# Sparse attention maps in a written-out order, gate weights loaded a chunk ahead, no GpSimd work among the mixers' weights

## The chip, the cores and the metric

The kernel runs on one core of a Trainium2 chip. A core has five engines with instruction queues of their own: PE (TensorE, matrix products), DVE (VectorE), ACT (ScalarE), POOL (GpSimd) and SP (SyncE, which here issues the DMAs). Each takes its instructions in order; an instruction that waits holds up all that stand behind it on its engine. The metric is device time in microseconds (us) of one execution; the kernel before takes 1821.24 us (median of 3 runs).

## The reference, cut to what matters

One decoder layer on 512 tokens of width 1024, in float32. The change is in its first part, two token mixers and their merge:

```python
u = rms_norm(h, norm_mix)
qa, ka, va, qb, kvb, gb, gate_a, gate_b = split(u @ w_in)
o_a = diff_attention(qa, ka, va, ...)      # 4 heads, two causal maps each: a = softmax(s0) - lam * softmax(s1)
o_b = nsa_attention(qb, kvb, sigmoid(gb))  # 8 heads in 2 groups: compressed, selected and window branch
#   o_b = g0 * o_cmp + g1 * o_slc + g2 * o_win      (with 8 blocks and top-16, all blocks are selected:
#   selected and window branch are plain causal attention with keys and values of their own)
merged = sigmoid(gate_a) * (o_a @ w_branch_a) + sigmoid(gate_b) * (o_b @ w_branch_b)
h = h + merged @ w_out
h = h + cross_attention(...); h = h + peer_ffn(...); out = rms_norm(h)
```

## The kernel before, in words

Every projection is done with operands split in two: `h` is the value rounded to TensorE's float32r, `l` the rest, and a product is three matmuls (`mm3`, lines 89 to 91: h·h, l·h, h·l). `split` (line 80) makes the pair: a cast on ACT and a subtraction on DVE, or on POOL for the weights whose running number stands in `WPOOL` and for the masks where a call says so. `wload` brings a weight chunk of 2048 columns in two halves: DMA to `wr`, cast to `wh`, subtraction to `wl`.

The mixers run in stages, the times being those of the profile. Norm and transposes of the input (to about 25 us); first projections and the hidden layer of the compressed keys (25 to 80); four differential heads (65 to 220, `diff_head`: two causal maps, the scaling P1 = P1·f (line 292) and P0 = P0·f − P1 (line 293), transposes (237), values (300), a head norm, transposes (309)), with the projections of the next head and of the sparse attention between them; the compressed map `nsa_cmp_map` (198 to 240); the sparse maps (`nsa_pair`, 201 to 372); the gates (`gate_half`, until 385); the merge with `w_br` (385 to 430). Behind that follow `w_out`, cross-attention and the expert layer, whose code is not touched.

A sparse map, for one head `r + 4g` and one branch `j`, is: four score rows of 128, 256, 384 and 512 columns (PE, line 216), each read out of PSUM by DVE with bias and row minimum (219), then exponential with row sum on ACT (220); the row factors on DVE (480, 481); the four rows scaled (487 on DVE, 485 on POOL for the rows named in `POOLM`: the third row, 384 columns); ten 128×128 transposes into three PSUM banks (PE, 237), each bank split by ACT (`PTh`) and DVE (`PTl`) (80); eight matmuls with the values (493) that add into the head's bank. After branch `j = 1` the two halves of the bank are added (`osum` on ACT, 496; add on DVE, 497). `nsa_pair` builds two heads at a time, with `GATE` halves of the gate projection (24 matmuls of 512 columns each) called between maps. Eleven of the sixteen gate halves are called there, five behind the last map; the results stay in SBUF (`gates`).

The order of instructions around here is not that of the code: outside `manual_schedule` blocks a scheduler with an estimate of durations orders the instructions of each engine, and interleaves what the dependencies allow.

Of the kernel before, what the change touches and what calls it, by code (L numbers as in the profile page):

```python
# [38 lines left out]
WPOOL = (1, 7, 9, 13, 15, 16, 17, 20, 21, 23, 38, 39, 42, 43)  # L39
DAF = ('cv', 'k', 'q', 'm')  # L40
# [3 lines left out]
POOLM = ((0, 2), (1, 2))  # L44
GATE = (3, 2, 1, 1, 1, 0, 1, 2)
# [14 lines left out]
class Kernel:  # L60
# [45 lines left out]
    def wload_parts(self, src, n=2048, eng=None):  # L106
# [9 lines left out]
        def half(c):  # L116
            r = wp.tile([P, w], F32, tag="wr", bufs=3, name=self.nm("wr"))
            nc.sync.dma_start(r, src[:, c:c + w])
            self.split(h[:, c:c + w], l[:, c:c + w], r, eng)
# [86 lines left out]
    def causal_maps(self, qk, biases):  # L206
# [4 lines left out]
        for i in range(NB):  # L211
            n, o, bl = P * (i + 1), ROW[i], slice(i * P, (i + 1) * P)
            sp = [self.bank("sc")[:, 0:n] for _ in qk]
            for s, (q, k) in zip(sp, qk):
                for y in range(2):
                    self.mark = nc.tensor.matmul(s, lhsT=q[:, bl], rhs=k[y][:, 0:n], start=y == 0, stop=y == 1)  # L216
# [6 lines left out]
    def causal_T(self, Pt, exact):  # L223
# [7 lines left out]
        for kbs, w in (((0,), 512), ((1, 3), 512), ((2,), 256)):  # L231
            pt = self.bank("pt")
# [18 lines left out]
    def diff_lambda(self, pool):  # L251
        nc = self.nc
        da = self.da
        lp = da.tile([P, 4, 64], F32, name="lamp")
        DQ(nc).dma_start(lp, self.a["lam"].unsqueeze(0).broadcast_to([P, 4, 64]))
        lt = da.tile([P, 2, 64], F32, name="lamt")
# [81 lines left out]
    def nsa_cmp_hidden(self, j, A, pool):  # L338
# [3 lines left out]
        ph = self.bank("pj")[0:32, 0:256]  # L342
# [6 lines left out]
        nc.scalar.activation(ge, ph, AF.Gelu)  # L349
        pt = self.bank("pt")  # L350
# [112 lines left out]
    def nsa_pair(self, r, fill):  # L463

        nc, dw = self.nc, self.dw
        hds, par = (r, r + 4), r % 2
        pr = slice(64 * par, 64 * par + 64)
        Bs = [self.bias(2.0 ** (-(hd + 1))) for hd in hds]
        po = [self.bank("po") for _ in hds]
        for hd, o in zip(hds, po):  # L470
            w = self.vc[:, hd].rearrange("p a b -> p (a b)")
            for y in range(2):
                nc.tensor.matmul(o, lhsT=w, rhs=self.pc[y], start=y == 0, stop=False)
        for j in range(2):
            maps = self.causal_maps([(self.qb[g][:, r, :], self.kb[j][g]) for g in range(2)], Bs)
            for _ in range(GATE[2 * r + j]):
                fill(self.mark)
            for g, (hd, o, (Pt, l)) in enumerate(zip(hds, po, maps)):
                f = dw.tile([P, NB], F32, tag="rl2", bufs=2, name=self.nm("rl"))
                nc.vector.reciprocal(f, l)  # L480
                nc.vector.tensor_tensor(f, f, self.gate[:, :, hd * 3 + 1 + j], OP.mult)
                for i in range(NB):
                    cs = slice(ROW[i], ROW[i] + P * (i + 1))
                    if (g, i) in POOLM:
                        nc.gpsimd.tensor_tensor(Pt[:, cs], Pt[:, cs], f[:, i:i + 1].broadcast_to([P, P * (i + 1)]), OP.mult)
                    else:
                        nc.vector.tensor_scalar(Pt[:, cs], Pt[:, cs], f[:, i:i + 1], None, OP.mult)
                T = self.causal_T(Pt, False)
                for kb in range(NB):
                    cs = slice(OFF[kb], OFF[kb] + S - kb * P)  # L490
                    w = self.vb[:, kb, j, g].rearrange("p z c -> p (z c)")
                    for y in range(2):
                        nc.tensor.matmul(o[:, kb * P:S], lhsT=w, rhs=T[y][:, cs], start=False, stop=(j, kb, y) == (1, NB - 1, 1))
        for hd, o in zip(hds, po):
# [14 lines left out]
    def mixers(self):  # L509
        nc, a = self.nc, self.a  # L510
        with ExitStack() as s1, ExitStack() as right:
# [30 lines left out]
            with ExitStack() as s2:  # L542
# [29 lines left out]
                for r in range(4):  # L572
                    self.nsa_pair(r, lambda m: self.gate_half(gp, m))
# [687 lines left out]
```

## Time and profile before

| | us |
|---|---|
| median of 3 runs (1819.18 to 1821.83) | 1821.24 |
| profiled execution | 1821.76 |
| its span on the core | 1820.0 |
| PE busy | 1753.3 (96%) |
| DVE busy | 1320.2 (73%) |
| ACT busy | 763.5 (42%) |
| POOL busy | 537.0 (30%) |

The ends of matmuls are modelled in this profile, so that a PE that is busy by the page need not be at its peak. The granted clock of TensorE is given as a share: 1.0 is the higher level (2.4 GHz), 0.50 the lower (1.2 GHz); its mean over the execution is 0.984. The stage in question is the first 430 us.

### The profile page before, as it was taken

The page shows a single profiled execution, that of the slowest core. Times are in us where ns is not written, and L with a number is a line of the kernel's source. Part 1 is how long each engine was busy: PE and PEld are TensorE (multiplying, and loading weights), DVE is VectorE, ACT ScalarE, POOL GpSimd, SP SyncE. Part 2 cuts the span into 40 slices and gives each one's busy share as a digit, 9 for nine tenths or more (in the row PEclk, how much of TensorE's full clock was granted, in tenths as well). Part 3 has the DMA queues.
Part 4 walks back from the last instruction along what each step waited for, and adds up shares of the span by engine and source line. Part 5 has one row for each costly group of instructions (what it writes and reads, how often), then busy time and mean ns, then how long its engine had stood idle before and what let it go on. Part 6 is the DMA issues. An engine that isn't in the chain of part 4 may idle for free.

```text
span 1820.0 us, 25916 instructions
## 1 busy us (share of the span) xinstructions
PE 1753.3 (96%) x9667; PEld 1550.2 (85%) x9667; DVE 1320.2 (73%) x2639; ACT 763.5 (42%) x1253; POOL 537.0 (30%) x386
## 2 busy tenths in 40 slices
PE   8999989999999999999999999999999999999998
PEld 7877777878987889998989888889888888888887
DVE  4465567555555899998873777778777787778777
ACT  4665446643454334454443333333233233323324
POOL 2211203100220251013210444344444444344442
PEclk8998989999999999999999999999999999999999
DMA  5521111035232224679999899999899989888994
GB/s 204 165 77 53 59 47 47 24 133 179 96 115 74 98 81 131 190 237 315 308 324 290 317 334 343 329 323 343 298 332 328 325 318 351 314 304 317 341 347 151
DMA packets 157967, 407.80 MB, mean 224 GB/s; under 512 B 13072, under 2 KB 62992, under 8 KB 157712
## 3 DMA queue, kind: packets, MB, share of 16 engines
q1 hardware_dynamic: 120976, 271.90, 42.9%
q0 software_dynamic: 36864, 134.23, 21.0%
q8 instruction: 76, 1.25, 0.3%
q14 instruction: 51, 0.42, 0.1%
HBM read 365.32 MB, written 39.71 MB: 223 GB/s over the span
## 4 chain that ended last, share of the span: by engine, by line
PE 68%; issue 12%; DVE 8%; DMA 5%; ACT 3%; POOL 3%; SPq 0%; DVEq 0%; POOLq 0%; ACTq 0%
PE pj L89 9%; PE pj L90 9%; PE pj L91 9%; PE sc L89 7%; PE sc L91 6%; PE sc L90 6%; PE po L91 3%; PE po L90 3%; PE po L89 3%; POOL gt L1038 2%; PE pt L90 2%; PE pt L91 2%; PE pt L89 2%; DMA gt<-in_peer_v,ex 2%; PE sc L216 1%
## 5 line engine op out<-in xcount | busy, mean ns | idle before, releaser
L89 PE MATMUL sc<-x,wh 128*128 128x384 f32 x1024 | 348.8, 341 | 8.7 <-ACT ge L808 7.8
L91 PE MATMUL sc<-x,wl 128*128 128x384 f32 x1024 | 348.3, 340 | 0.1
L90 PE MATMUL sc<-x,wh 128*128 128x384 f32 x1024 | 347.4, 339 | 0.3 <-DVE x L80 0.3
L1038 POOL DMA_INDIRECT gt<-in_peer_u,ex x128 | 202.4, 1581 | 442.0 <-DVE gt L1047 315.1
L80 ACT CAST wh<-wr 128x1024 fp32r<-128x1024 f32 (+1 forms) x230 | 227.3, 1020 | 187.9 <-DMA wr<-in_ut 63.9
L80 DVE TENSOR_TENSOR wl<-wr,wh 128x1024 fp32r<-128x1024 f32 (+2 forms) x188 | 216.8, 1178 | 66.8 <-ACT wh L80 66.6
L1038 POOL DMA_INDIRECT gt<-in_peer_v,ex x128 | 189.3, 1479 | 253.3 <-DVE acc L1056 221.2
L80 ACT CAST w<-ge 128x768 fp32r<-128x768 f32 (+1 forms) x65 | 53.6, 825 | 386.1 <-DVE ge L1116 377.6
L80 DVE TENSOR_TENSOR v<-vr,v 128x1024 fp32r<-128x1024 f32 x128 | 151.4, 1223 | 88.3 <-ACT v L80 88.2
L89 PEld LDWEIGHTS sc<-x,wh 128*128 128x128 f32 x1024 | 193.8, 189 | 12.0 <-ACT ge L808 9.0
L90 PEld LDWEIGHTS sc<-x,wh 128*128 128x128 f32 x1024 | 193.9, 189 | 2.1 <-DVE x L80 0.5
L91 PEld LDWEIGHTS sc<-x,wl 128*128 128x128 f32 x1024 | 193.9, 189 | 0.4 <-DVE wl L80 0.4
L1047 DVE SCALAR_TENSOR_TENSOR gt<-gt,xg 128x1024 f32<-128x1024 f32 x128 | 151.7, 1222 | 27.8 <-DMA gt<-in_peer_u,ex 27.8
L1056 DVE SCALAR_TENSOR_TENSOR acc<-gt,ag,acc 128x1024 f32<-128x1024 f32 x127 | 162.9, 1283 | 11.9 <-DMA gt<-in_peer_v,ex 9.3
L80 ACT CAST v<-vr 128x1024 fp32r<-128x1024 f32 x128 | 128.3, 1049 | 84.9 <-PE pj L91 83.5
L80 POOL TENSOR_TENSOR wl<-wr,wh 128x1024 fp32r<-128x1024 f32 x42 | 101.6, 2438 | 125.5 <-ACT wh L80 82.4
L89 PE MATMUL pj<-uh,wh 128*128 128x512 f32 x256 | 103.9, 406 | 3.1 <-ACT gates L507 1.6
L80 DVE TENSOR_TENSOR w<-ge,w 128x768 fp32r<-128x768 f32 (+1 forms) x65 | 61.5, 946 | 58.1 <-ACT w L80 55.4
L90 PE MATMUL pj<-ul,wh 128*128 128x512 f32 x256 | 103.2, 403 | 0.0
L91 PE MATMUL pj<-uh,wl 128*128 128x512 f32 x256 | 103.2, 404 | 0.0
L89 PE MATMUL po<-v,w 128*128 128x512 f32 x256 | 100.0, 391 | 1.9 <-ACT w L80 1.8
L91 PE MATMUL po<-v,w 128*128 128x512 f32 x256 | 100.2, 391 | 1.0 <-DVE w L80 1.0
(366 smaller groups left out, 3823.6 us busy)
## 6 DMA issues: line engine op xcount, KB each, us to landing
wr<-in_ut SPq DMA_DIRECT2D x128, 512.0 KB
vr<-in_peer_v SPq DMA_DIRECT2D x128, 512.0 KB
Gd<-Gs SPq DMA_DIRECT2D x48, 512.0 KB
G<-Gd SPq DMA_DIRECT2D x31, 768.0 KB
wr<-in_w_in SPq DMA_DIRECT2D x36, 512.0 KB
Ad<-ge SPq DMA_DIRECT2D x29, 384.0 KB
ge<-Ad SPq DMA_DIRECT2D x29, 384.0 KB
wr<-in_w_pq SPq DMA_DIRECT2D x16, 512.0 KB
```

Of the source, the lines that this page charges most:

```text
L80: return nc.scalar.copy(h, src), (eng or nc.vector).tensor_tensor(l, src, f32(h), OP.subtract)
L89: first = mm(out, lhsT=lh, rhs=rh, start=start, stop=False)
L90: mm(out, lhsT=lh, rhs=rl, start=False, stop=False)
L91: mm(out, lhsT=ll, rhs=rh, start=False, stop=stop)
L216: self.mark = nc.tensor.matmul(s, lhsT=q[:, bl], rhs=k[y][:, 0:n], start=y == 0, stop=y == 1)
L1038: self.nc.gpsimd.indirect_dma_start(g, None, tab, bass.IndirectOffsetOnAxis(ap=self.ex[:, s % P:s % P + 1], axis=0))
L1047: i = v.scalar_tensor_tensor(g, g, 1.0, self.xg, OP.mult, OP.mult, accum_out=ag[:, s:s + 1])
L1056: v.scalar_tensor_tensor(acc, g, ag[:, s - P:s - P + 1], acc, OP.mult, OP.add)
```

## The change

Three things. First, POOL: `WPOOL` names only weights of the cross stage now, so the twenty subtractions of mixer weights that POOL did (two for each of ten weights) are done by DVE, and so are the sixteen row scalings of `POOLM`.

Second, the gates: `gates()` is a generator that yields after every nine matmuls and after each half. Heads 0, 1 and 3 of the differential attention run one chunk (two halves) each behind their maps; the remaining five chunks are the filling of the sparse maps. Their weights come a chunk ahead there: the DMAs of the next chunk are issued when a chunk begins, its casts and subtractions after the first half. Results go to DRAM (`gd`) through a staging tile and come back in the merge (`g`). The four branches of other work after the heads change their order (`DAF`).

Third, `nsa_maps`: the sixteen sparse maps ("units" below) stand in a written-out order, one unit ahead: two score rows of the next unit, a piece of gate matmuls, the eight first transposes of this unit, the two other rows of the next, a piece of gate matmuls, the last two transposes, the values (key block 2 last), for `j = 1` the add, then the scaling of the next unit. A half's last piece has six matmuls.

```diff
...
-WPOOL = (1, 7, 9, 13, 15, 16, 17, 20, 21, 23, 38, 39, 42, 43)
-DAF = ('cv', 'k', 'q', 'm')
+WPOOL = (38, 39, 42, 43)
+DAF = ('cv', 'q', 'm', 'k')
...
-POOLM = ((0, 2), (1, 2))
-GATE = (3, 2, 1, 1, 1, 0, 1, 2)
+GATED = (0, 1, 3)
...
-        def half(c):
+        def raw(c):
             r = wp.tile([P, w], F32, tag="wr", bufs=3, name=self.nm("wr"))
             nc.sync.dma_start(r, src[:, c:c + w])
+            return r
+
+        rs = {c: raw(c) for c in (0, w)} if ahead else {}
+
+        def half(c):
+            r = rs.get(c) or raw(c)
             self.split(h[:, c:c + w], l[:, c:c + w], r, eng)
...
         for kbs, w in (((0,), 512), ((1, 3), 512), ((2,), 256)):
+            if fill and kbs == (2,):
+                fill()
             pt = self.bank("pt")
...
-    def nsa_pair(self, r, fill):
+    def nsa_maps(self, ob, fill):
...
+            for kb in (0, 1, 3, 2):
+                cs = slice(OFF[kb], OFF[kb] + S - kb * P)
+                w = self.vb[:, kb, j, g].rearrange("p z c -> p (z c)")
+                for y in range(2):
+                    nc.tensor.matmul(o[:, kb * P:S], lhsT=w, rhs=T[y][:, cs], start=False, stop=(j, kb, y) == (1, 2, 1))
+            if j == 1:
+                t = dw.tile([P, S], F32, tag="on", bufs=2, name=self.nm("osum"))
+                nc.scalar.copy(t[0:64], o[64:128, :])
+                nc.vector.tensor_tensor(ob[hd // 2][64 * (r % 2):64 * (r % 2) + 64, :], o[0:64, :], t[0:64], OP.add)
+
+        next(fill, 0)
+        with self.tc.manual_schedule():
+            m = begin(*units[0])
+            for i in range(NB):
+                row(units[0], m, i)
+            scale(units[0], m)
+            for u, n in zip(units, units[1:] + [None]):
+                if n:
+                    mn = begin(*n)
+                    row(n, mn, 0)
+                    row(n, mn, 1)
+                next(fill, 0)
+
+                def mid():
+                    if n:
+                        row(n, mn, 2)
+                        row(n, mn, 3)
+                    next(fill, 0)
+
+                T = self.causal_T(m[0], False, mid)
+                values(u, T)
+                if n:
+                    scale(n, mn)
+                    m = mn
+            for _ in fill:
+                pass
+
+
+    def gates(self):
...
+            for j in range(2):
+                o, cs = self.bank("pj"), slice(j * P, (j + 1) * P)
+                for k in range(KT):
+                    self.mm3(o, wh[:, k, cs], wl[:, k, cs], self.U[0][:, k, :], self.U[1][:, k, :], k == 0, k == KT - 1)
+                    if k % 3 == 2:
+                        yield
+                t = self.dw.tile([P, S], F32, tag="gh", bufs=1, name=self.nm("gh"))
+                nc.scalar.copy(t, o)
+                nc.sync.dma_start(self.gd[d][:, j], t)
+                if j == 0 and nxt:
+                    for f in nxt[1]:
+                        f()
+                    nxt = nxt[0], ()
...
-                    self.diff_head(hd, qk, lambda: nxt.extend(self.diff_qk(da, hd + 1) if hd < 3 else ()))
+
+                    def then():
+                        if hd == 0:
+                            ge[:] = [self.nsa_cmp_T(z) for z in ge]
+                        if hd < 3:
+                            nxt.extend(self.diff_qk(da, hd + 1))
+                        if hd in GATED:
+                            n = self.ngate + 1
+                            for _ in self.gates():
+                                if self.ngate == n:
+                                    break
+
+                    self.diff_head(hd, qk, then)
...
-                while self.ngate < 16:
-                    self.gate_half(op)
...
-                    g = self.gates[d]
+                    g = op.tile([P, 2, S], F32, tag="g", bufs=3, name=self.nm("g"))
+                    nc.sync.dma_start(g, self.gd[d])
```

DVE's order in the sparse stage of the kernel before, at a place where a gate weight is split (`wl` is the weight's rest, `PTl` that of a transposed map, `st` the row minima and sums, `rl` the row factors):

```order
L487 TENSOR_SCALAR P_2063<-P_2063,rl_2170 128x128
L487 TENSOR_SCALAR P_2063<-P_2063,rl_2170 128x256
L487 TENSOR_SCALAR P_2063<-P_2063,rl_2170 128x512
L487 TENSOR_SCALAR P_2064<-P_2064,rl_2206 128x128
L487 TENSOR_SCALAR P_2064<-P_2064,rl_2206 128x256
L487 TENSOR_SCALAR P_2064<-P_2064,rl_2206 128x512
L80 TENSOR_TENSOR PTl_2035<-pt_2050,PTh_2034 128x256
L80 TENSOR_TENSOR wl_2445<-wr_2446,wh_2444 128x1024
L80 TENSOR_TENSOR wl_2445<-wr_2450,wh_2444 128x1024
L219 ISA P_2258,st_2260<-sc_2262,B_2248 128x128
L219 ISA st_2260 128x1
L80 TENSOR_TENSOR PTl_2178<-pt_2179,PTh_2177 128x512
```

The rows of two maps are scaled one map after the other (the third row is not here, POOL does it), and the last `PTl` and the weight's two subtractions stand behind the scaling.

The same engine of the changed kernel, fourth unit, where the weight of the next gate chunk is split:

```order
L492 ISA P_2354,st_2355<-sc_2396,B_2352 128x512
L492 ISA st_2355 128x1
L79 TENSOR_TENSOR wl_2314<-wr_2315,wh_2313 128x1024
L79 TENSOR_TENSOR wl_2314<-wr_2317,wh_2313 128x1024
L79 TENSOR_TENSOR PTl_2376<-pt_2414,PTh_2375 128x256
L520 TENSOR_TENSOR ob_2040<-po_2248,osum_2427 64x512
L498 RECIPROCAL rl_2430<-st_2355 128x4
L499 TENSOR_TENSOR rl_2430<-rl_2430,gate 128x4
L502 TENSOR_SCALAR P_2354<-P_2354,rl_2430 128x128
L502 TENSOR_SCALAR P_2354<-P_2354,rl_2430 128x256
L502 TENSOR_SCALAR P_2354<-P_2354,rl_2430 128x384
L502 TENSOR_SCALAR P_2354<-P_2354,rl_2430 128x512
```

Both subtractions now stand between the last two rows of the next unit and the `PTl` of this one's last transposes; the add of the finished head and the whole scaling, with the third row, come behind that.

TensorE of the kernel before, the values of a map of the sparse stage (`pj` is a gate half, `po` the head's bank, `pt` a bank of transposes):

```order
L237 MATMUL pt_2387<-cB,P_2259 128x128 x2
L493 MATMUL po_2253<-PTl_2372,vb_987 128x512
L493 MATMUL po_2253<-PTh_2371,vb_987 128x384
L91 MATMUL pj_2455<-uh,wl_2445 128x512
L89 MATMUL pj_2455<-uh,wh_2444 128x512
L90 MATMUL pj_2455<-ul,wh_2444 128x512
L91 MATMUL pj_2455<-uh,wl_2445 128x512
L89 MATMUL pj_2455<-uh,wh_2444 128x512
L493 MATMUL po_2253<-PTl_2372,vb_987 128x384
L90 MATMUL pj_2455<-ul,wh_2444 128x512
L91 MATMUL pj_2455<-uh,wl_2445 128x512
```

Gate matmuls stand between the values of one map.

TensorE of the changed kernel, from the end of a piece of gate matmuls to the next score row:

```order
L244 MATMUL pt_2496<-cB,P_2354 128x128 x2
L510 MATMUL po_2501<-pcT_1778,vc_1046 128x512
L510 MATMUL po_2501<-pcT_1779,vc_1046 128x512
L516 MATMUL po_2501<-PTh_2461,vb_1060 128x512
L516 MATMUL po_2501<-PTl_2462,vb_1060 128x512
L516 MATMUL po_2501<-PTh_2461,vb_1060 128x384
L516 MATMUL po_2501<-PTl_2462,vb_1060 128x384
L516 MATMUL po_2501<-PTh_2461,vb_1060 128x128
L516 MATMUL po_2501<-PTl_2462,vb_1060 128x128
L516 MATMUL po_2501<-PTh_2461,vb_1060 128x256
L516 MATMUL po_2501<-PTl_2462,vb_1060 128x256
L491 MATMUL sc_2521<-kb_2022,qb_1419 128x128
```

The values of a unit now follow the last two transposes with nothing between them; a unit's gate matmuls stand ahead of the first and of the last transposes.

SP's DMA queue of the kernel before, at the end of the sparse stage (`or` are the outputs of the differential heads, `h` the residual rows, `w_br` the merge weights):

```order
L591 DMA or_3365<-od_74 128x512
L591 DMA or_3369<-od_75 128x512
L591 DMA or_3373<-od_76 128x512
L118 DMA wr_3437<-in_w_br 128x512
L579 DMA h_3187<-in_x 128x1024
L579 DMA h_3188<-in_x 128x1024
L579 DMA h_3189<-in_x 128x1024
L579 DMA h_3190<-in_x 128x1024
L118 DMA wr_3475<-in_w_br 128x512
L591 DMA or_3377<-od_77 128x512
```

And of the changed kernel (`gd` and `g`: a gate written to DRAM, and read back):

```order
L571 DMA gd_85<-gh_3282 128x512
L672 DMA or_3399<-od_74 128x512
L672 DMA or_3403<-od_75 128x512
L672 DMA or_3407<-od_76 128x512
L662 DMA h_3373<-in_x 128x1024
L662 DMA h_3374<-in_x 128x1024
L662 DMA h_3375<-in_x 128x1024
L662 DMA h_3376<-in_x 128x1024
L677 DMA g_3433<-gd_78 128x1024
L677 DMA g_3477<-gd_79 128x1024
L677 DMA g_3521<-gd_80 128x1024
L672 DMA or_3411<-od_77 128x512
```

The fourth `or` is now behind four `h` of 512 KB and three `g` of 512 KB.

## Rows read from the trace of the kernel before

**Rows 1.** windows: width; busy PE, PEld, DVE, ACT, POOL; clock, DMA share, GB/s

```profile
68.00:200.00 132.00, 119.58 (x619) 98.92 (x618) 77.40 (x158) 84.35 (x159) 32.62 (x21) 0.95 0.27 91
200.00:244.00 44.00, 35.33 (x158) 28.09 (x158) 23.17 (x59) 15.55 (x39) 3.79 (x4) 0.84 0.15 53
244.00:385.00 141.00, 135.24 (x713) 113.07 (x712) 90.81 (x252) 87.82 (x203) 26.01 (x20) 0.99 0.16 59
385.00:430.00 45.00, 45.00 (x198) 36.59 (x197) 30.63 (x47) 17.00 (x27) 0.00 (x0) 1.00 0.38 124
72.20:75.60 3.40, 3.40 (x16) 2.75 (x17) 1.62 (x6) 3.35 (x8) 0.00 (x0) 0.50 0.48 171
137.10:143.90 6.80, 5.42 (x13) 4.26 (x14) 2.28 (x5) 4.36 (x9) 0.00 (x0) 0.50 0.01 2
378.00:384.00 6.00, 6.00 (x27) 4.90 (x27) 1.35 (x2) 1.27 (x3) 0.00 (x0) 1.00 0.98 388
```

**Rows 2.** groups by shape, PE, 68 to 200: busy, mean ns, idle before

```profile
L89 PE MATMUL pj<-uh,wh 128*128 128x512 f32 x96 | 39.8, 415 | 1.5 <-ACT dkh L204 1.5
```

**Rows 3.** the same, 200 to 244

```profile
L436 PE MATMUL pt<-cB,pc 128*128 128x128 f32 x4 | 1.1, 428 | 3.7 <-DVE pc L433 3.7
```

**Rows 4.** the same, 244 to 385

```profile
L89 PE MATMUL pj<-uh,wh 128*128 128x512 f32 x104 | 41.0, 395 | 1.6 <-ACT gates L507 1.6
...
L237 PE MATMUL pt<-cB,P 128*128 128x128 f32 x155 | 25.4, 282 | 1.5 <-DVE P L487 0.8 <-DVE PTl L80 0.6
```

**Rows 5.** the chain of waits, 160 to 172: start, us, what

```profile
163.25 3.47 DVE P L292 x4
166.72 3.99 DVE P L293 x4
```

**Rows 6.** the chain of waits, 200 to 205

```profile
202.96 1.19 DVE P L292 x4
```

**Rows 7.** the chain of waits, 260 to 263

```profile
261.31 0.87 PE pt L237 x8
```

**Rows 8.** timeline, 126 to 139: start, us, engine, line, operation

```profile
128.74 5.05 POOL L80 TENSOR_TENSOR wl<-wr,wh 128x1024 fp32r<-128x1024 f32 x2 [4.18 <-ACT wh L80]
...
129.04 6.22 DVE L293 SCALAR_TENSOR_TENSOR P<-P,rl,P 128x128 f32<-128x128 f32 x4
...
138.48 0.79 PE L89 MATMUL pj<-uh,wh 128*128 128x512 f32 x1 [1.51 <-ACT dkh L204]
```

**Rows 9.** groups by line and shape, POOL, 0 to 440

```profile
L80 POOL TENSOR_TENSOR wl<-wr,wh 128x1024 fp32r<-128x1024 f32 x20 | 48.7, 2453 | 84.4 <-DVE dkl L203 43.1 <-ACT wh L80 41.3
L485 POOL TENSOR_TENSOR P<-P,rl 128x384 f32<-128x384 f32 x16 | 13.5, 851 | 101.1 <-DVE rl L481 99.3 <-ACT PTh L80 1.0 <-PE pt L237 0.8
...
L129 POOL TENSOR_TENSOR rstd<-rstd,mhalf 128x4 f32<-128x4 f32 x4 | 4.0, 1012 | 67.1 <-DVE rstd L128 67.1
```

**Rows 10.** groups by line and shape, DVE, 201 to 372

```profile
L80 DVE TENSOR_TENSOR wl<-wr,wh 128x1024 fp32r<-128x1024 f32 x6 | 7.2, 1221 | 1.8 <-ACT wh L80 1.8
...
L80 DVE TENSOR_TENSOR PTl<-pt,PTh 128x256 fp32r<-128x256 f32 x16 | 6.7, 416 | 8.4 <-ACT PTh L80 8.4
...
L497 DVE TENSOR_TENSOR ob<-po,osum 64x512 f32<-64x512 f32 x7 | 4.8, 681 | 5.1 <-ACT osum L496 5.1
...
L480 DVE RECIPROCAL rl<-st 128x4 f32<-128x4 f32 x16 | 2.5, 168 | 0.2
...
L306 DVE TENSOR_TENSOR osq<-po,rstd 128x512 f32<-128x512 f32 x1 | 0.7, 692 | 0.4 <-POOL rstd L129 0.4
```

**Rows 11.** groups by line and shape, ACT, 201 to 372

```profile
L80 ACT CAST wh<-wr 128x1024 fp32r<-128x1024 f32 x12 | 12.0, 1047 | 17.0 <-PE pj L90 11.7 <-issue 5.3
...
L507 ACT COPY gates<-pj 128x512 f32<-128x512 f32 x12 | 6.9, 586 | 20.7 <-PE pj L91 17.5 <-DVE pc L433 3.1
...
L80 ACT CAST PTh<-pt 128x256 fp32r<-128x256 f32 x16 | 5.9, 369 | 10.1 <-PE pt L237 10.1
L496 ACT COPY osum<-po 64x512 f32<-64x512 f32 x7 | 4.1, 583 | 3.4 <-PE po L493 3.3
```

More of the change, by code (lines that the diff above doesn't have):

```diff
@@ L461, in nsa_v @@
             self.split(vb[:, :, 0], vb[:, :, 1], o)
-    def nsa_pair(self, r, fill):
+    def nsa_maps(self, ob, fill):
         nc, dw = self.nc, self.dw
[L466 to L471, printed above, removed]
-            for y in range(2):
[L473 to L494, printed above, removed]
-            t = dw.tile([P, S], F32, tag="on", bufs=2, name=self.nm("osum"))
-            nc.scalar.copy(t[0:64], o[64:128, :])
-            nc.vector.tensor_tensor(self.ob[hd // 2][pr, :], o[0:64, :], t[0:64], OP.add)
@@ L500, in gate_half, with begin @@
-    def gate_half(self, pool, after=None):
-        d, j = divmod(self.ngate, 2)
-        self.ngate += 1
-        if j == 0:
-            self.gW = self.wload(self.a["w_in"][10 + d])
-            self.gates.append(pool.tile([P, 2, S], F32, name=f"gates{d}"))
-        self.nc.scalar.copy(self.gates[d][:, j, :], self.proj_T(self.gW, j * P, *self.U, S, after=after))
+        units = [(r, j, g) for r in range(4) for j in range(2) for g in range(2)]
+        B, po = {}, {}
+        def begin(r, j, g):
+            if j == 0:
+                B[g] = self.bias(2.0 ** (-(r + 4 * g + 1)))
+            return dw.tile([P, 1280], F32, tag="P", bufs=PB, name=self.nm("P")), dw.tile([P, 2, NB], F32, tag="st", bufs=4, name=self.nm("st"))
@@ new lines, in nsa_maps @@
+        next(fill, 0)
+        with self.tc.manual_schedule():
+            m = begin(*units[0])
+            for i in range(NB):
+                row(units[0], m, i)
[18 more added lines that the diff above has]
+                pass
@@ new lines, in gates @@
+    def gates(self):
+        nc = self.nc
+        load = lambda d: self.wload_parts(self.a["w_in"][10 + d], ahead=self.ahead) if d < KT else None
+        nxt = load(self.ngate)
+        while self.ngate < KT:
+            d = self.ngate
+            W, half = nxt
+            if half:
+                for f in half:
+                    f()
+            nxt = load(d + 1) if self.ahead else None
+            wh, wl = (w.rearrange("p (k c) -> p k c", c=256) for w in W)
+            for j in range(2):
[9 more added lines that the diff above has]
+                    for f in nxt[1]:
+                        f()
+                    nxt = nxt[0], ()
+                if j == 1:
+                    self.ngate += 1
+                yield
@@ L515, in mixers @@
             self.od = [dp.tile([P, S], F32, name=f"od{i}") for i in range(4)]
+            self.gd, self.ngate, self.ahead = [dp.tile([P, 2, S], F32, name=f"gd{d}") for d in range(KT)], 0, False
             with ExitStack() as s2:
```

46 lines of the change are left out of this document (35 added, 11 removed).

## The prediction

> **What bounds the kernel now.** I read the stage table first [rows 1]. From 385 to 430 us TensorE does nothing but matmuls of 512 columns, 198 in 45.0 us, so one costs 0.227 us; a dense run of eight transposes takes 0.87, so 0.109 each [rows 7]. With these, and narrower matmuls in proportion to their columns, I worked out for each stretch what PE needs if it never waits. From 68 to 200: 312 matmuls of 512 columns (the projections' 96 on each of three lines [rows 2] and 24 of the maps and the compressed map) are 71 us, the other 307 about 35, so 106 of 132 us: 26 us are rest. From 200 to 244 it is 28 of 44, rest 16. From 244 to 385 it is 386 wide ones (104 on each of three lines), 155 transposes [rows 4] and 172 narrow matmuls at about 0.11: 88 + 17 + 19 = 124 of 141, rest 17. From 385 to 430: none. So PE bounds these stages, and about 59 us in them are not its work. That rest is what the change can win or make larger.
>
> Three causes show in it. DVE is held by POOL: in the timeline two POOL subtractions run from 128.74 for 5.05 us and beside them four DVE operations take 6.22 [rows 8]; in the chain the four first scalings take 3.47 at 163 us [rows 5] and 1.19 at 203, without POOL [rows 6]. The clock falls: the mean of 0.95 over 68 to 200 is 13 us at half speed, of which 6.8 from 137.1 on [rows 1], with waits the last of which ends at 138.48, after 1.51 us [rows 8]. And chains through several engines have nothing to cover them: 3.7 us ahead of the compressed map's second transposes, for DVE [rows 3].
>
> **Part 1, POOL's work to DVE.** Twenty subtractions of 2.45 us and sixteen scalings of 0.85 leave POOL [rows 9]. DVE gets 20 × 1.22 = 24 us [rows 10] and 16 × 0.4 = 6 us (an estimate: four scalings take 1.19 [rows 6], and this is the second largest). DVE is busy 77 of 132 and 91 of 141 us [rows 1], so these 30 us fit, as long as they don't stand on a chain. What goes is the holding: 6.14 less about 2 at 129 us, 7.46 (3.47 + 3.99 [rows 5]) less about 3.3 at 163: some 8 us on the chain, and with them waits of PE that the clock's falls follow.
>
> The Trainium skill has a rule for this ("SBUF — State Buffer", "Who interferes with whom"): DVE and GpSimd share one pair of ports as an exclusive lock, and the loser blocks for the other's whole instruction. By it each of the eight subtractions of the heads could hold DVE for its full length, at most 8 × 2.45 = 20 us; the trace shows two such places and about 8 us, and I go by these.
>
> **Part 2, six gate halves in the heads.** A half is 24 matmuls, 5.4 us; six bring 33 us of PE work to 68 to 200, out of the later stages, to stand beside the scaling, the head norm and the weights' splits. With 8 us of holding gone, some 4 of clock, and about 4 of other waits covered, the rest of the heads falls from 26 to 10: −16 us. What stays is the wait for the compressed keys' hidden layer at 72 us (the clock falls there too [rows 1]), whose transposes stand at the same place in the order. Bounds: −22 (rest 4) and −6 (the holding alone, less what DVE's own work gives back). The passage from the last head to the first sparse unit now has the compressed map a head earlier, which takes away the 3.7 us; the last head's norm (ACT, DVE, POOL, DVE, together 3 to 3.5 us by POOL's 1.01 [rows 9] and DVE's 0.69 [rows 10]) and the first unit's scaling, which has no unit ahead of it, stay. Rest 10 for 16: −6, bounds −9 and 0.
>
> **Part 3, the sparse units.** PE needs in a unit ten transposes, 1.1 us, eight row matmuls 1.15, eight of the values 1.15, and fifteen or eighteen gate matmuls, 3.4 to 4.1: about 7.0 to 7.5. DVE needs about 6 (83 us without the weights for the 14 units from 244 on [rows 1]), so a plain unit is PE's. Two kinds are not.
>
> Four units split a gate weight (place 1 of the orders shown). From the end of the piece of six, ACT copies the half (0.586), casts twice (2 × 1.05) and only then makes the last `PTh` (0.37) [rows 11]; DVE does the second subtraction behind the second cast (1.22) and then the last `PTl` (0.42) [rows 10]. With hand-overs: 0.1 + 0.59 + 2.09 + 1.22 + 0.42 = 4.4 us. Beside it PE has two transposes and six value matmuls, 1.1. So it waits 3.3 us for the last two values; 3.5, as the last exponential may still run when the piece ends. Four times: 14.
>
> In the eight units with `j = 1` the next scaling stands behind the add: osum 0.58 [rows 11], add 0.68, reciprocal and factor 0.33 [rows 10], four rows 1.19 [rows 6], hand-overs 0.2, in all 3.0 from the last value to the transposes, beside two rows and nine (six) matmuls, 2.4 (1.7): waits of 0.6 to 1.3, seven in all 7 (the last has no successor). The last unit has no filling: 5. Waits for the last `PTl`, which stands behind two exponentials and in every third unit behind a gate copy too, I put at half a us in each unit: 8. Sum 34, for 17 before: +17; the stage is then 144 us with 110 of PE's work. Bounds: +28 if every unit is as slow as the `j = 1` ones, and −8 (rest 9) if three in four of these waits have work beside them that I don't see.
>
> Four waits of 3.5 us may lower the clock. The trace has both: at 72.2 the half clock lies in the wait itself and costs next to nothing, from 137.1 it lasts 5.4 us past the wait's end at 138.5 and costs half of that, 2.7 [rows 1, 8]. I take 1 each, +4, bounds 0 and +11.
>
> **Part 4, into the merge.** Before, five gate halves cover the loads and splits of the merge's inputs, with 1.6 us of PE's waits [rows 4]. Now the merge begins at once, with `ob`; its operands take the room of the sparse stage's tiles, so the first split waits for the last osum and add (1.26 [rows 10, 11]), with hand-overs 1.5. The fourth `or` (place 3) lands behind 4.5 MB, 11.6 us at the 388 GB/s of 378 to 384 [rows 1], with start and split 14; until then PE has 42 matmuls, 9.5 us. 14 − 1.5 − 9.5 = 3 us of wait. In all 4.5 for 1.6, and a little for the gates' way back: +3.5, bounds 0 and +6. The writes of the gate halves on SP's queue are hidden by the matmuls of the next half. The start, up to 68 us, changes by one POOL split: 0, bounds −1 and +2.
>
> **Sum.** −16 − 6 + 17 + 4 + 3.5 = +2.5 us, on the profiled execution's 1821.76; its distance to the median, 0.5, I leave as it is: 1821.24 + 2.5 = 1823.7. Behind 430 us nothing changes.
>
> **Rivals.**
> R1, slower: the weight split sets the pace of four units and the clock pays for it. Each wait of 3.5 us ends in 3.4 us or more at 1.2 GHz, which costs 2.7 as at 137 us, and the piece of gate matmuls that should cover the next scaling comes later by that. For it: the fall at 137 follows waits that are single no longer than these. Against: a unit bound by DVE's chain hides part. +17 becomes +21 to +24, clock +11: 1821 − 22 + 22.5 + 11 + 3.5 = 1836. It decides if the half clock shows behind all four. The Trainium skill says ("TensorE: Matmul & The Clock Gate", Part 1) that an idle PE falls to 1.2 GHz and has to be busy to come back; the stretches at 0.50 agree.
> R2, faster: the waits in the units are mostly covered (exponentials and copies sooner than the rows say, the osum chain 1 us shorter), so that the stage keeps its 17 us, while heads and passage win the 22: 1821 − 22 + 3.5 = 1803. For it: without POOL four scalings take 1.19 and not up to 3.47 [rows 5, 6], on every chain; against: the order above is fixed, ACT and DVE can't pass the split.
> R3, the change does not do what it says: the weights' DMAs ended none of the long waits here, so asking a chunk ahead hides nothing, and DVE's 30 us take back what POOL's holding cost. The heads win 6, the units lose 6: 1821.
>
> **How the numbers follow.** My forecast 0.46, R1 0.18, R2 0.30, R3 0.06. The forecast's own range is 1815 to 1832. Within 0.2% (what a measurement here can tell from no change, 3.6 us) lies 0.21 of its 0.46, 0.18 above, 0.07 below. R1 is slower, R2 faster, R3 the same. Faster 0.37, same 0.27, slower 0.36. The range takes in most of R1 and R2: 1799 to 1838.
>
> **What would show it.** In the profile after: no DVE scaling above 0.8 us before 430; rest of PE about 10 us in the heads; units that repeat at 7 to 8 us, four of 11 to 13, with PE's wait named `PTl` and ahead of that a cast of `wh`; a wait of about 3 us for the split of the fourth `or`; half clock behind some of the four. Wrong would be the forecast if the four units show no wait of 2 us or more (R2), or if the heads keep a rest above 20 us.

## The result: slower by 1.2%, and the profile after

The changed kernel takes 1842.79 us (median of 4 runs, 1839.41 to 1845.94), the kernel before in the same comparison 1820.21; the ratio is 1.0117 with a 95% interval of 1.0102 to 1.0133. The forecast was 1823.7 with a range up to 1838. It had the sign right, but forecast a change of 2.5 us where 22.6 were measured, and the time lies outside the range.

The windows by stage of the profile after (columns as in [rows 1]; the sparse stage ends at 395 now, the merge at 449), and four of its stretches at half clock:

```profile
68.00:200.00 132.00, 128.67 (x681) 109.72 (x682) 74.38 (x147) 79.09 (x145) 5.21 (x8) 0.99 0.33 113
200.00:243.00 43.00, 37.56 (x176) 30.94 (x175) 26.04 (x72) 22.23 (x52) 2.02 (x2) 0.84 0.09 31
243.00:395.00 152.00, 126.55 (x628) 102.56 (x626) 91.14 (x273) 73.41 (x189) 0.00 (x0) 0.92 0.16 51
395.00:449.00 54.00, 49.34 (x193) 38.71 (x193) 34.11 (x52) 27.43 (x39) 0.00 (x0) 0.89 0.65 227
273.70:280.50 6.80, 3.93 (x11) 3.18 (x12) 4.74 (x10) 2.47 (x4) 0.00 (x0) 0.50 0.10 39
304.40:311.20 6.80, 5.45 (x15) 4.39 (x16) 5.16 (x15) 1.38 (x6) 0.00 (x0) 0.50 0.00 1
386.30:400.00 13.70, 9.63 (x29) 7.03 (x29) 8.43 (x18) 6.03 (x11) 0.00 (x0) 0.50 0.25 85
410.20:417.00 6.80, 5.53 (x12) 3.94 (x13) 4.24 (x8) 3.48 (x6) 0.00 (x0) 0.50 0.16 56
```

The next table has TensorE's rest in each stage, in us: the stage's width less what TensorE needs without a wait, from the count of matmuls by shape and the intervals of [rows 1, 7], as in the prediction. Each rest is that of one profiled execution.

| kernel | heads (68 to 200) | passage | sparse maps | merge |
|---|---|---|---|---|
| before | 26.9 | 16.7 | 16.9 | 1.4 |
| forecast | 10 | 10 | 34 + 4 | 5 |
| changed | 9.6 | 13.4 | 48.1 | 10.6 |

The heads did what was forecast: PE did 681 matmuls there, not 619, at a mean clock of 0.99, not 0.95. Their scalings are no longer held as those of [rows 5, 8] were. This shows in the groups by line and shape (DVE, 68 to 240; mean ns behind the busy time), before:

```profile
L293 DVE SCALAR_TENSOR_TENSOR P<-P,rl,P 128x128 f32<-128x128 f32 x4 | 5.7, 1418 | 0.0
...
L292 DVE TENSOR_SCALAR P<-P,rl 128x512 f32<-128x512 f32 x4 | 4.1, 1028 | 0.0
```

and in the changed kernel, where these lines are 299 and 298:

```profile
L299 DVE SCALAR_TENSOR_TENSOR P<-P,rl,P 128x512 f32<-128x512 f32 x4 | 3.0, 746 | 0.0
...
L298 DVE TENSOR_SCALAR P<-P,rl 128x512 f32<-128x512 f32 x4 | 1.9, 481 | 0.0
...
L299 DVE SCALAR_TENSOR_TENSOR P<-P,rl,P 128x128 f32<-128x128 f32 x4 | 1.4, 347 | 0.0
```

The widest of line 299 take the 746 ns that they took before too; the gain is in the first scalings of a group.

What was lost is in the sparse maps, and some in the merge. The timeline of the changed kernel at the second weight split (start, duration, engine, line, operation; in brackets the idle time before it and what ended it):

```profile
271.57 0.22 PE L516 MATMUL po<-PTh,vb 128*128 128x128 f32 x1
...
272.14 0.72 ACT L493 ACTIVATE P<-P,st 128x512 f32<-128x512 f32 x1
...
272.86 0.56 ACT L570 COPY gh<-pj 128x512 f32<-128x512 f32 x1
273.32 1.99 ACT L79 CAST wh<-wr 128x1024 fp32r<-128x1024 f32 x2
...
274.40 2.36 DVE L79 TENSOR_TENSOR wl<-wr,wh 128x1024 fp32r<-128x1024 f32 x2 [2.30 <-ACT wh L79]
275.21 0.37 ACT L79 CAST PTh<-pt 128x256 fp32r<-128x256 f32 x1
...
275.64 0.58 PE L516 MATMUL po<-PTh,vb 128*128 128x256 f32 x1 [3.73 <-ACT PTh L79]
276.68 0.42 DVE L79 TENSOR_TENSOR PTl<-pt,PTh 128x256 fp32r<-128x256 f32 x1
...
277.15 0.58 PE L516 MATMUL po<-PTl,vb 128*128 128x256 f32 x1 [0.93 <-DVE PTl L79]
...
278.38 0.63 PE L88 MATMUL pj<-uh,wh 128*128 128x512 f32 x1
...
278.81 0.63 PE L89 MATMUL pj<-ul,wh 128*128 128x512 f32 x1
```

The chain is the one worked out: gate copy, two casts, then `PTh`; the second subtraction, then `PTl`. TensorE waits 3.73 and 0.93 us; most of the wait is named `PTh` and not, as forecast, `PTl`. The next gate matmuls (278.38, 278.81) start 0.43 us apart where they start 0.23 apart at full clock. The four splits' waits are 2.3, 4.7, 3.7 and 3.4 us, 14.1 in all. By group they and the waits of the other units are (idle before, and what ended it, in the last column; changed kernel, 243 to 395):

```profile
L244 PE MATMUL pt<-cB,P 128*128 128x128 f32 x152 | 24.9, 288 | 5.2 <-DVE P L502 2.8 <-DVE PTl L79 2.1
...
L516 PE MATMUL po<-PTl,vb 128*128 128x256 f32 x16 | 6.7, 421 | 4.5 <-DVE PTl L79 4.1
...
L516 PE MATMUL po<-PTh,vb 128*128 128x256 f32 x16 | 6.4, 398 | 14.8 <-ACT PTh L79 14.8
```

In the merge the fourth output of the heads is late as forecast (timeline, changed kernel):

```profile
410.80 0.60 ACT L79 CAST oh<-or 128x512 fp32r<-128x512 f32 x1
...
411.45 1.22 PE L88 MATMUL sc<-oh,wh 128*128 128x512 f32 x2 [3.45 <-ACT oh L79]
```

A wait of 3.45 us for 3 forecast, but the half clock behind it (the row of 410.2 above) had not been put in the sum.

### The profile page after: what moved, and what is told of

It is laid out like the page before. It is cut to its first block, busy times and chain, and to the rows that moved or that the text cites. A ratio compares the mean times of both kernels' runs of the same rounds, so it can differ in the third digit from the quotient of the medians.

```text
span 1844.2 us, 25929 instructions
## 1 busy us (share of the span) xinstructions
PE 1764.1 (96%) x9667; PEld 1559.5 (85%) x9667; DVE 1327.6 (72%) x2675; ACT 763.2 (41%) x1253; POOL 474.7 (26%) x350
## 4 chain that ended last, share of the span: by engine, by line
PE 68%; issue 11%; DVE 8%; DMA 5%; ACT 4%; POOL 2%; SPq 0%; DVEq 0%; ACTq 0%; POOLq 0%
PE pj L88 9%; PE pj L89 9%; PE pj L90 9%; PE sc L88 7%; PE sc L90 7%; PE sc L89 7%; PE po L90 3%; PE po L89 3%; PE po L88 3%; PE pt L89 2%; PE pt L90 2%; PE pt L88 2%; POOL gt L1120 2%; DMA gt<-in_peer_u,ex 2%; DVE wl L79 2%
## 5 line engine op out<-in xcount | busy, mean ns | idle before, releaser
L79 DVE TENSOR_TENSOR wl<-wr,wh 128x1024 fp32r<-128x1024 f32 (+2 forms) x208 | 239.8, 1179 | 94.5 <-ACT wh L79 94.3
L79 ACT CAST wh<-wr 128x1024 fp32r<-128x1024 f32 (+2 forms) x230 | 226.9, 1020 | 180.9 <-DMA wr<-in_ut 57.9
L1138 DVE SCALAR_TENSOR_TENSOR acc<-gt,ag,acc 128x1024 f32<-128x1024 f32 x127 | 162.9, 1282 | 13.7 <-DMA gt<-in_peer_v,ex 11.3
L134 POOL TENSOR_TENSOR rstd<-rstd,mhalf 128x1 f32<-128x1 f32 (+1 forms) x22 | 14.9, 676 | 448.2 <-DVE rstd L133 444.8
```

Source lines behind the costliest of these rows:

```text
L79: return nc.scalar.copy(h, src), (eng or nc.vector).tensor_tensor(l, src, f32(h), OP.subtract)
L134: nc.gpsimd.tensor_tensor(r, v, self.mhalf[:, 0:n], OP.pow)
L1138: v.scalar_tensor_tensor(acc, g, ag[:, s - P:s - P + 1], acc, OP.mult, OP.add)
```

## The experiments

Each was compared with the kernel before in the same session; ratios are to that kernel, with a 95% interval. The differences between runs given below are those of their medians; going by the intervals they are known to some 3 to 6 us, so that 1 to 3 us between two runs are not clear of the noise.

One figure of a trace leaves out the code behind the mixers: the time at which the merge's last matmul ends. It is 429.3 us in the kernel before and 449.1 in the changed one.

### Part 1 alone on the kernel before

```diff
-WPOOL = (1, 7, 9, 13, 15, 16, 17, 20, 21, 23, 38, 39, 42, 43)
+WPOOL = (38, 39, 42, 43)
-POOLM = ((0, 2), (1, 2))
+POOLM = ()
```

> The kernel before with part 1 alone: POOL does none of the twenty weight subtractions of the mixers and none of the sixteen row scalings; DVE does them. Theory: the changed kernel's heads (68 to 200 us) lost 17 us of TensorE's rest, and half of that or more is POOL no longer holding DVE: 1809 to 1813 us, with no four scalings above 1.3 us and fewer half-clock stretches. Rival: it was the gate halves in the heads that did it, and DVE's 30 us more come back as new waits: 1817 to 1824 us.

1811.07 us, ratio 0.9949 (0.9930 to 0.9968): 9.6 us faster, as the theory had it. The rest in the heads falls to 22.4 and in the passage to 11.8; in the sparse stage, where the clock no longer falls, it stays at 16.8:

```profile
68.00:200.00 132.00, 121.59 (x650) 102.28 (x651) 84.45 (x185) 84.28 (x169) 6.15 (x9) 0.96 0.28 97
...
230.50:374.00 143.50, 137.44 (x726) 114.17 (x725) 93.67 (x272) 88.32 (x203) 0.00 (x0) 1.00 0.17 56
```

DVE does 84 us of work in the heads for 77 before, and PE still gets through more there, 650 matmuls for 619; POOL is at 6 us for 33. The scalings that were held are short in this run too: 345 ns on line 293 with 128 columns, for 1418, and 480 on line 292 with 512, for 1028. The rule of the Trainium skill quoted in the prediction ("SBUF — State Buffer", "Who interferes with whom") has the hold right. The upper bound of 20 us that the prediction worked out for the heads was far off: their rest fell by 4.5, and all stages together gave 9.6.

### The gate weights not split

```diff
-            nxt = load(d + 1) if self.ahead else None
+            nxt = None
+            if self.ahead and d + 1 < KT:
+                ...               # the two DMAs of the next chunk alone
+                nxt = W, ()
```

> The changed kernel without casts and subtractions of the gate weights of chunks 4 to 7 (their DMAs stay; the gates are computed with chunk 3's weights, so the output differs). Theory: the four waits for the last PTh and PTl (14.1 us in the trace after) and the half clock behind three of them (about 6 us) go: 1842.8 - 20 = 1823 us. Rival: the units are bound by their next chain anyway (scaling behind the add, exponentials ahead of PTh), and only 8 us go: 1835 us.

1830.69 us, ratio 1.0060 (1.0044 to 1.0077): 12 us of the 20 that the theory gave. The four waits are gone, but others of the same kind have grown in their place, in units that split no gate weight:

```profile
L516 PE MATMUL po<-PTh,vb 128*128 128x256 f32 x16 | 6.2, 390 | 9.9 <-ACT PTh L79 9.9
```

9.9 us of waits for the last `PTh`, none of which stands behind a gate weight; the stage's rest is 36.1. So the splits are 12 of the 31 us lost in this stage, waits and clock together (18 in the forecast), and the plain units are slow too. Two units hold a split that the written-out order does not show: the scheduler puts those of the merge's first two weights into the stage, at 322.8 and 370.5 us in this run, at 351.7 and 380.5 in the changed kernel (two subtractions, 1.3 to 1.45 us on DVE, each time). How much it costs was not tested.

### Scaling ahead of the add

```diff
                 if n:
                     scale(n, mn)
                     m = mn
+                finish(u)          # osum and add, taken out of values()
```

> The changed kernel with the next unit's scaling ahead of the add of a finished head (both instructions of the add moved behind the scaling). My step of the prediction put 7 us on the scaling behind the add: 1836 us. Theory after the trace: the waits named for a scaling are 2.8 us in all, most of them in the last unit, and the waits for the last PTh (ACT) decide: 1840 us, 1 to 3 us less than the changed kernel.

1836.54 us, ratio 1.0091 (1.0074 to 1.0108): 6.2 us less than the changed kernel. That is near my step of the prediction (7 us); the second reading, 1 to 3 us from the waits that bear the scaling's name (2.8 us), was too small. The trace agrees: the merge's last matmul ends at 442.3, 6.8 us earlier.

### The heads' part without the written-out maps

The sparse maps are those of the kernel before (two heads at a time, in the scheduler's order), without POOL, with eight of the ten remaining gate halves between them and two behind; all else as changed.

```diff
-                self.ahead = True
-                self.nsa_maps(self.ob, self.gates())
+                self.nhalf = 2 * self.ngate
+                for r in range(4):
+                    self.nsa_pair(r, lambda m: self.gate_half(self.dw, m))
```

> The changed kernel with the sparse maps of the kernel before (two heads at a time, order left to the scheduler, all scalings on DVE), eight of the ten remaining gate halves between them and two behind them; gates through DRAM as in the changed kernel. Theory: the written-out order is what costs, the heads keep their 17 us: 1803 to 1808 us. Rival: gate halves that are spent in the heads are missing in the sparse stage, whoever orders it, and it loses 10 us or more there: 1813 to 1822 us.

1813.19 us, ratio 0.9957 (0.9940 to 0.9973): within the rival's range, at its lower end. The sparse stage and the merge of this run (windows):

```profile
240.00:363.90 123.90, 117.93 (x646) 97.64 (x644) 88.25 (x270) 73.48 (x187) 1.01 (x1) 1.00 0.13 44
363.90:419.30 55.40, 49.16 (x193) 38.60 (x194) 34.14 (x52) 28.49 (x42) 0.00 (x0) 0.91 0.69 237
```

Rests: heads 9.6, passage 12.9, sparse 17.5, merge 11.7. Against the run without POOL (22.4, 11.8, 16.8, 1.1) the changed heads save 13 us, and they cost 1 in the sparse stage, 1 in the passage and 11 in the merge. So the stage that lacks the gate halves loses next to nothing, other than the rival had it; the merge pays. Its DMAs and first splits have lost the cover of all five halves, for the scheduler puts the two last ones among the last map's work: the last gate matmul starts at 361.0 us, the last value at 363.6, and then TensorE waits 1.80 and, for the fourth output, 4.42 us. (The changed heads hold the gate halves, the later transposes of the compressed keys' hidden layer and the new order behind the heads; these were not taken apart.) The written-out order, with the places that it gives the splits, costs 48.1 − 17.5 = 31 us.

### The merge's queue, alone

```diff
-            for b in range(NB):
-                DQ(nc).dma_start(self.h[b], a["x"][b * P:(b + 1) * P, :])
...
-op.tile([P, S], F32, tag="or", bufs=3, name=self.nm("or"))
+op.tile([P, S], F32, tag="or", bufs=4, name=self.nm("or"))
...
                     self.split(O[0][:, i, :], O[1][:, i, :], t)
+                for b in range(NB):
+                    DQ(nc).dma_start(self.h[b], a["x"][b * P:(b + 1) * P, :])
```

> The changed kernel with a fourth buffer for the differential heads' outputs and the loads of h behind them in the queue. Theory: the wait of 3.45 us for the fourth output and the half clock behind it (2.8 us) go: 1842.8 - 6 = 1837 us. Rival: the loads of the gates or of the merge weights, now later, end the same wait: 1842 us.

1837.95 us, ratio 1.0082 (1.0051 to 1.0112): 4.9 us less; the merge's rest goes from 10.6 to 5.1, by the wait of 3.45 and the half clock behind it. What is left is 1.19 us at its start and the half clock that the last unit hands over.

### The split spread over two units

```diff
...                # in nsa_maps, behind scale()
+                if self.todo:
+                    self.todo.pop(0)()
...                # in gates
                 if j == 0 and nxt:
-                    for f in nxt[1]:
-                        f()
+                    if self.ahead:
+                        self.todo.extend(nxt[1])
...
```

> The changed kernel with the two halves of a gate weight's split at the ends of two units (behind the next unit's scaling) instead of both ahead of the last transposes' split. Leaving the split out took 12 us. Theory: at a unit's end a half of it (cast 1.05, subtraction 1.22) still delays the chain through ACT and DVE, by about 1 us each, eight times: 4 to 6 us less than the changed kernel, 1837 to 1839 us. Rival: the unit's end is free on both engines, all 12 us go: 1831 us.

1834.77 us, ratio 1.0071 (1.0048 to 1.0094): 8.0 us less, between the two; a third of what a split costs stays at the units' ends.

### Score rows behind the transposes

```diff
-                if n:
-                    mn = begin(*n)
-                    row(n, mn, 0)
-                    row(n, mn, 1)
                 next(fill, 0)
...                # in mid(): begin, rows 0 and 1, a gate piece
                 T = self.causal_T(m[0], False, mid)
+                if n:
+                    mn = nxt[0]
+                    row(n, mn, 2)
+                    row(n, mn, 3)
```

> The changed kernel with one thing moved: the first two score rows of the next unit (and its bias) stand behind the eight first transposes of this one, the two others behind its last transposes, so that on ACT and DVE the splits of a unit's transposes no longer wait behind the next unit's exponentials. Theory from the trace after: a unit without a weight split repeats at 7.6 to 10.5 us because the splits stand behind exponentials, these behind row reads and these behind the scaling on the other engine; with the order turned the chain is about 8 us for each unit, and the four splits keep their waits: 1842.8 - 10 to 16 = 1827 to 1833 us. Rival: the units are bound by DVE's sum of work, and nothing moves: 1839 to 1845 us.

1840.23 us, ratio 1.0110 (1.0089 to 1.0131): 2.6 us less, in the rival's range and not clear of the noise; in its trace the merge ends at 450.3, no earlier than in the changed kernel. In its trace the waits for `PTh` of plain units are gone and TensorE waits for scalings instead, four times 0.7 to 2.3 us within the stage and 3.4 ahead of the last unit.

### Three mends together, and the rows behind as well

> The changed kernel with three edits of the runs before together: scaling ahead of the add (6.2 us less alone), a weight split's halves at the ends of two units (8.0), four buffers for the heads' outputs with h behind them (4.9). Theory: they act at different places and add: 1842.8 - 19 = 1824 us. Rival: the first two shorten the same chain through ACT and DVE, so that only the longer counts: 1829 to 1833 us.

1823.87 us, ratio 1.0012 (1.0000 to 1.0024): 18.9 us less, for the 19.1 to which the three savings add. As each of these is known to some 4 to 6 us only, the close fit is partly luck.

> The same three edits, and the next unit's first two score rows behind the eight first transposes as well. Alone that edit took only 2.6 us, as the waits moved to the scaling behind the add (about 5 us of waits for a scaling in its trace). Theory: with the scaling ahead of the add these go: 5 to 7 us less than the three edits alone, 1817 to 1819 us. Rival: one unit ahead is too little whatever the order within it: within 2 us of the three edits.

1817.18 us, ratio 0.9980 (0.9967 to 0.9994): 6.7 us less again, as the theory had it. Alone the rows' place gave nothing that stands clear of the noise, as the waits went over to the scaling; with the scaling ahead of the add these are gone too. Up to the last unit the stage then holds its clock (windows, this run, to 369 us and to the stage's end):

```profile
243.60:369.00 125.40, 117.66 (x612) 93.20 (x610) 88.49 (x269) 73.18 (x190) 0.00 (x0) 1.00 0.19 61
243.60:374.60 131.00, 120.88 (x626) 95.58 (x625) 92.51 (x279) 75.62 (x195) 0.00 (x0) 0.99 0.18 59
```

The stage's rest is 27.1, for 48.1.

### One term out of the chain: no scaling

```diff
-            for i in range(NB):
-                cs = slice(ROW[i], ROW[i] + P * (i + 1))
-                nc.vector.tensor_scalar(p[:, cs], p[:, cs], f[:, i:i + 1], None, OP.mult)
```

> The changed kernel without the four row scalings of each sparse map (the factors are still made; the outputs are not normalised). It takes 1.2 us of DVE out of every unit, at the place between the exponentials and the transposes. Theory: a unit is bound by one chain through the engines (scaling, transposes, splits, row reads, exponentials), which gets shorter by these 1.2 us: 16 x 1.0 to 1.2 = 16 to 19 us less, 1824 to 1827 us. Rival: TensorE's own work binds the units without a weight split, and only waits that show as idle before a transpose (2.8 us) go: 1837 to 1840 us.

1837.27 us, ratio 1.0078 (1.0050 to 1.0107): 5.5 us less, not 16 to 19, and in the rival's range. So the theory of one chain through the scaling of every unit is refuted. I read it so: the scaling is on the longest path only of units where it stands behind an add, as the third run had it; the others are held at `PTh`, behind the exponentials, and waits of 0.8 to 1.4 us for it remain in this trace.

### What holds the pace when the mends are in

The run with 1817.18 us has no wait above 1 us ahead of its last unit, and yet its units take 7.2 to 9.9 us each, for the 7.0 to 7.5 that TensorE needs. These are its waits (243 to 369 us; total, times, longest):

```profile
PE sc L491 <- DVE st L492: 3.0, 7, 0.9
PE pt L244 <- DVE P L502: 1.7, 5, 0.7
PE pt L244 <- DVE PTl L79: 1.1, 2, 0.8
```

They sum to 6 us of the some 23 that TensorE has of rest there; the others show as no wait. The same run without the gate weights' split:

> The same run (three mends and rows behind, 1817.2) without casts and subtractions of the gate weights of chunks 4 to 7 (their DMAs stay, the output differs). Theory: what still keeps its units at 8 to 9.5 us, with no wait above 1 us in the stage, is DVE's sum of work: eight subtractions of 1.22 fewer give 7 to 10 us, 1807 to 1810 us. Rival: the chain of a single unit ahead holds the pace, the split lies beside it: 1815 to 1817 us.

1814.78 us, ratio 0.9966 (0.9953 to 0.9978): 2.4 us less, which is not clear of the noise and far from the theory's 7 to 10. From the first unit to the stage's end DVE has 8.5 us less to do (84.0 for 92.5), and the stage is 1.3 us shorter, 129.7 for 131.0:

```profile
243.10:372.80 129.70, 120.64 (x628) 96.40 (x627) 84.02 (x271) 68.30 (x187) 0.00 (x0) 0.99 0.18 59
```

So DVE's sum does not set the pace. That the path of a map does, with only one unit ahead, fits with these short waits, for a row read here and a scaling there, but it is not shown: no run had two units ahead.

### Where the gate halves are best spent, and the best kernel

> The changed heads with the sparse maps as before, eight gate halves between the maps and two behind them, and the merge's loads mended (four buffers, h behind them): the run with 1813.2 us plus the queue edit alone. Theory: 4.4 us of wait and some half clock go: 1807 to 1808 us, a little less than with four halves behind the maps (1809.2), as the sparse stage keeps two more to fill with. Rival: with two halves to cover them the merge's first splits wait for other loads: 1811 to 1813 us.

1811.82 us, ratio 0.9943 (0.9922 to 0.9964): 1.4 less than without the queue edit, the rival's range, and not clear of the noise. In its trace the merge's rest falls from 11.7 to 7.7, which is not nothing, but much stays: here too the last gate matmul (363.9) stands ahead of the last value (366.4), so that no half covers the loads.

> The kernel with the changed heads and the sparse maps as before, with the merge mended: four buffers for the heads' outputs, h behind them, and four gate halves behind the last map instead of two. Theory: the merge's rest falls from 8 to about 2 us, the sparse stage keeps 20: 1813.2 - 6 = 1807 us. Rival: two gate halves less between the maps cost there what they save: 1813 us.

1809.15 us, ratio 0.9938 (0.9914 to 0.9962): with four halves behind the maps gate matmuls run until 367.2 us, 7 us past the last value, and the merge's rest is 1.4.

> The run with the three mends and the rows behind (1817.2), with a chunk of gates in two heads only (0 and 1) instead of three, so that the sparse units' filling lasts past the last unit and covers the merge's first loads. Theory: the last unit's waits and the merge's rest (about 5 us each) shrink, the last head gets 4 us of rest back: 1812 to 1814 us. Rival: a gate half is worth the same wherever it fills, 1817 us.

1811.66 us, ratio 0.9950 (0.9932 to 0.9968): 5.5 less, as the theory had it. The last unit and the merge (rest 1.3) are covered, and the written-out order is as fast as the scheduler's with two halves behind it.

> The best kernel so far (changed heads, sparse maps as before, merge mended, 1809.2) with gates in two heads, eight halves between the sparse maps and four behind. Theory: two halves more fill the sparse stage (rest 24.7 there) and the last head loses as much: 1807 to 1811 us. Rival: the last head's waits come back whole: 1813 us.

1807.58 us, ratio 0.9930 (0.9906 to 0.9954): the best, 0.7% below the kernel before. Sparse maps in the scheduler's order, POOL out of the mixers, gates in two heads, eight halves between the maps and four behind; the merge is at its own pace (windows, 364 to 414: 217 matmuls of 512 columns in 50.0 us):

```profile
68.00:200.00 132.00, 128.54 (x677) 109.56 (x678) 75.91 (x151) 80.69 (x148) 5.22 (x8) 0.97 0.32 111
...
230.00:364.00 134.00, 125.56 (x683) 104.63 (x682) 94.61 (x278) 80.83 (x199) 1.01 (x1) 0.99 0.19 61
364.00:414.00 50.00, 50.00 (x217) 40.58 (x216) 27.26 (x44) 24.05 (x35) 0.00 (x0) 1.00 0.67 233
```

Its distance to the run with 1809.15 (1.6 us) is within the two intervals. Its distance to part 1 alone is 3.5 us by the ratios, known to some 6. So of the best kernel's gain the times show no more than POOL's part for certain.

## Why the prediction was wrong

The step that failed is in part 3: "so a plain unit is PE's. Two kinds are not." With it failed the clock's term, 4 us. The stage's rest was put at 34 us, and 4 for the clock; it is 48, clock included. Without the four splits the sum leaves 20, and the run without them keeps 36.

Right were: the heads, −16 forecast and −17.3 measured (26.9 to 9.6), of which POOL's part is 4.5 there (9.6 over all stages, part 1 alone) and the other changes of the heads, the gate halves above all, 12.8; the waits at the four splits, 14 forecast and 14.1 in the trace; the scaling behind the add, 7 for 6.2; the wait for the fourth output, 3 for 3.45.

Mis-sized were three terms. First the plain units. I had compared sums, DVE's 6 us with PE's 7.0 to 7.5, and gave half a microsecond a unit to what stands in between. I expected units that repeat at 7 to 8 us; from the last value matmul of one to that of the next, the ten repeats without any weight's split take 7.5 to 10.3, in the mean 9.0. With one unit ahead and engines that take their instructions in order, `PTh` stands behind exponentials on ACT, and these behind row reads on DVE: I take it that a path through both engines, longer than either's work, binds these units. Three runs bear on it: leaving out the splits took 12 us, not 18, and left 9.9 us of waits for `PTh`; the rows behind the transposes took 6.7 us once the other mends were in; and what was left did not depend on DVE's sum (2.4 us for 8.5 us of work). But the scaling, which such a path would have to pass if it ran from unit to unit, is not on it in most units (5.5 us, not 16 to 19), so where the path closes stays open.

Second the clock: after the splits' waits it fell three times of four, and in the last unit and the merge, where I had counted none, for 13.7 us from 386 and 6.8 from 410; a wait of 3.45 us there costs 4.9 to 5.5 with what follows it. The matmuls that ran at half clock need, by the intervals of [rows 1, 7], 8.4 us at full clock in the sparse stage and 4.8 in the merge. That much the clock cost (an estimate), for 4 and nothing in the sum: 9 of the 16 us that are missing in these two stages. The 1 us that I took for each fall rested on a misreading of the row at 72.2 [rows 1]. The half clock there does not lie in the wait: TensorE is busy for all of its 3.40 us. The timeline of the kernel before (PE) has the wait's end ahead of it and matmuls of 256 columns 0.21 us apart in it, for 0.12 behind it:

```profile
71.85 0.31 PE L352 MATMUL pt<-cB,ge 32*128 32x32 f32 x2 [3.62 <-ACT ge L349]
...
74.97 0.41 PE L89 MATMUL pj<-wh,A 128*32 128x256 f32 x1
75.18 0.41 PE L90 MATMUL pj<-wl,A 128*32 128x256 f32 x1
...
75.73 0.28 PE L90 MATMUL pj<-wl,A 128*32 128x256 f32 x1
75.85 0.28 PE L91 MATMUL pj<-wh,A 128*32 128x256 f32 x1
```

So that fall cost some 1.6 us, and not next to nothing.

Third the passage, 13.4 for 10: the head norm's wait stayed and the clock fell twice in it. These are +10 (sparse, clock included), +5.6 (merge) and +3.4, less 0.4 in the heads: 18.6 of the 20 us that were missing. Behind the merge, where I had put nothing, the changed kernel's trace takes 1395.0 us, that of the kernel before 1390.7. The code there is the same in all runs, and their traces show 1387.0 to 1395.2, so this may be no more than the spread of single executions.

The rivals: R1 named the half clock (behind three of the four, not all) and the split, in the right place, but its 1836 was not far enough, since it took the plain units for fast as well. R2's reason (waits covered) is refuted by the trace after. Of R3, the heads' half is refuted.

The gains need no written-out order. POOL out of the mixers gives 9.6 us. The gate halves' 13 us in the heads are paid back, 12 us, nearly all in the merge, which loses its cover, unless it keeps four of them.

## What to carry to other kernels

A written-out order is to be judged by the path of one item through all engines, not by each engine's sum alone: write, for each engine, what stands ahead of the instruction that the next engine waits for, and follow it around once. An operation with a long chain of its own (here a weight's split, cast and subtraction) goes behind what others wait for, not ahead of it. Filling is a store: a matmul that fills one stage is missing in another, so look for the stage where its absence costs least, and keep some for the place where loads begin.

## What the runs showed of the hardware

TensorE's clock fell to half around single waits of 3 to 4 us: with the wait of 3.73 us that ended at 275.64 it stood at 0.50 from 273.7 to 280.5, so for 4.9 us past the wait. It also fell with shorter waits close together: from 338.5 to 341.9 with 2.30 and 1.13 us, from 386.3 on behind 1.50 and 1.35. In the run with the rows behind and three mends, with no wait above 1 us, it stayed at full for the 125 us up to the last unit.

POOL's subtractions hold DVE's scalings: with them the four of 128 columns on line 293 took 1418 ns in the mean, without them 345. Giving them to DVE made both the heads and the passage faster, with 7 us more work on DVE in the heads.
